# A two-layer encoder trunk in split float32: all 22 channel blocks of the down-projection in the seven-product form

## The chip, the cores and the metric

The kernel runs on one core of one Trainium2 chip. The metric is the device time of one execution, in microseconds (us). Five engines of the core appear below: TensorE (PE; its weight loads are PEld), VectorE (DVE), ScalarE (ACT), GpSimd (POOL) and SyncE (SP). SP and POOL only issue transfers in the stages treated here. Each engine works through its own list of instructions in a fixed order.

## The reference

Two layers, 512 tokens of 1024 channels, float32. A layer is a mixing block (four branches: convolution and three kinds of attention) and then a convolutional feed-forward block. The change concerns the feed-forward block alone:

```
D_MODEL = 1024
SEQ = 512
D_FF = 2816
def _conv_ffn(h, w_up, conv_w, conv_b, w_down):
    u = _depthwise_conv(h @ w_up, conv_w, conv_b)       # width 3 along the tokens
    gate, up = jnp.split(u, 2, axis=-1)
    return (jax.nn.silu(gate) * up) @ w_down
...
        x = x + _conv_ffn(_rmsnorm(x, g_ffn[l]), w_up[l], ffn_conv_w[l], ffn_conv_b[l], w_down[l])
```

So the down-projection is a product of a 512 x 2816 matrix and a 2816 x 1024 one, in each layer.

## The kernel before

**Split float32.** Every float32 operand `x` is cut into `hi = round(x)` in TensorE's reduced float32 (by ACT) and `lo = x - hi` (by DVE), and a product is three matmuls: hi·hi, hi·lo, lo·hi. A matmul works on 128 rows of the contraction and 512 output columns. Weights are cut on the way in: `weights()` loads a unit of 128 x 1024 (512 KB) by SP into a tile `w_raw`, ACT makes `w_hi` of it, DVE makes `w_lo`. There are three `w_hi` and three `w_lo` buffers, so the `w_hi` of a unit can only be made once TensorE has finished the unit three before it. The scheduler gives this work a priority 3000 instructions ahead of its place; where each instruction then stands on its engine is fixed when the program is built.

**Up-projection (`ffn`).** It loops over 22 channel blocks `i`. For each, two units (gate and value half) of 24 matmuls go into two of four PSUM banks `mm`. DVE multiplies the bank by the norm's factors (`U<-mm,RB`), ACT and DVE do the width-3 convolution (`cy`), ACT takes silu (`fth`), DVE multiplies the halves into `fl`, a 128 x 512 tile of the hidden activations. `RB` is known only some time after the first units are done, since it goes through DRAM.

**Down-projection (`down`).** In before, two of the 22 hidden blocks (NK = 2, `kind 'rows'`) are multiplied directly: two units of 24 matmuls, into eight banks. The other 20 go in NP2 = 10 pairs through the seven-product (Strassen-Winograd) scheme. A pair of blocks is a 2 x 2 arrangement of quarters, and seven products of sums of quarters take the place of eight. This needs

- sums of quarters of the weights (`weight_sums`): per pair DVE does four 128 x 512 operations on the two tiles `quad`; POOL has loaded these (two transfers) and stores the results to DRAM (four transfers, `sums`). It runs beside the up-projection, once for every second channel block;
- sums of quarters of the activations, cut into hi and lo (`split_pair`): per pair ACT does three 128 x 512 operations and one of 256 columns, DVE three of 512 and five of 256. In before, four pairs (`EARLY = 4`) are cut beside the up-projection and six in the down-projection.

The first phase of the seven-product form takes two units of 12 matmuls per pair, into eight banks A, B, C, E of 128 x 512 (two of each). In the second phase three of the sums go on to grow, A (`a12`), E (`a22`) and C (`s4`), with one unit of 12 matmuls per two pairs; between them DVE and ACT combine the banks into the result `xt`. In layer 0, `update` then turns the result back and prepares the next layer's norm; in the last layer, the residual (`resT`) is added and `store` writes the output.

**What sets the order on SP.** All loads of `w_raw` stand on SP in one list, with the loads of the residual in the last layer. The weights of the down-projection use four buffers in turn, two named `w_raw` and two named `w_more`; the two `w_more` are the same memory as `quad`, so they become free when the last sums have been stored.

Of the kernel before, what the change touches and what calls it, by code (L numbers as in the profile page):

```python
# [31 lines left out]
NP2 = 10  # L32
NK = NF - 2 * NP2

EARLY = 4
# [28 lines left out]

ORDER = (1, 2, 3, 0)
# [5 lines left out]
def weight_units():  # L71
# [20 lines left out]
    units.extend(('rows', (k0, h), 1024) for h in range(2) for k0 in range(0, NK, 2))  # L92
    units.extend(('quad', NK + 2 * j, 2048) for j in range(NP2))
# [7 lines left out]
def pack_weights(w_in, w_branch, w_out, w_up, w_down):  # L101
    out = np.empty((L, WLEN), np.float32)
    for l in range(L):
        off = 0
        for kind, a, n in UNITS:
# [9 lines left out]
            elif kind == 'rows':  # L115
                k0, h = a
                src = w_down[l][k0 * P:(k0 + 2) * P, h * 512:(h + 1) * 512].reshape(2, P, 512).transpose(1, 0, 2)
# [73 lines left out]
class Trunk:  # L191
# [7 lines left out]
    def weights(self, upto, ahead=3000, parts=1, queue=None):  # L199

        nc = self.nc
        while self.w_emitted < min(upto, len(self.w_list)):
            n, pieces = self.w_list[self.w_emitted]
            with self.tc.high_priority(offset=ahead):
                if n == 0:

                    n = 1024
# [5 lines left out]
                src = pieces()  # L213
                if len(src) == 1:
# [649 lines left out]
    def ffn(self, l, last):  # L864
# [3 lines left out]
        for i in range(4):  # L868
            u = self.fp.tile([P, 514 + (4 * PHASE if i == 3 else 0)], F32, name=f"U{i}", tag=f"U{i}", bufs=1)
# [5 lines left out]
        for i in range(NF):  # L875
# [39 lines left out]
            if i >= NK + 4 and (i - NK) % 4 == 0 and j < EARLY:  # L915
                self.split_pair(F, j, self.got)
# [20 lines left out]
    def last_units(self, l):  # L937
# [7 lines left out]
        for f in (lambda j: quad(j, 2), lambda j: sums(j, 3, 4), lambda j: quad(j, 3)):  # L945
            units.extend(lambda f=f, j=j: [f(j), f(j + 1)] for j in range(0, NP2, 2))
        self.w_list.extend((1024 * (n % 4 < 2), u) for n, u in enumerate(units))
# [7 lines left out]
    def weight_sums(self, l, j):  # L955
# [3 lines left out]
        t3, t2 = (self.fp.tile([P, S], F32, name=f"t{n}", tag=f"s4{n}{j % 2 * 2}", bufs=1) for n in 'hl')  # L959
# [10 lines left out]
    def pair_tags(self, j):  # L970
# [3 lines left out]
        i = NK + 2 * j  # L974
        x = [f"x{n}{d}" for d in range(KT) for n in 'hl']
        own = [f"fh{i}", f"fh{i + 1}"]
        late = [f"fh{NF - 6 + n}" for n in range(6)]
        hi = {NP2 - 3: x[12:14], NP2 - 2: x[14:16], NP2 - 1: ["fh1", "fl1"]}.get(j, own)
        lo = ["lo", "lo"] if j == 0 else [f"fl{i - 2}", f"fl{i - 1}"]
        a = (["e0", "e1"], ["e2", "e3"], late[0:2], late[2:4])[j] if j < EARLY else x[2 * (j - EARLY):][:2]  # L980
        s4 = (["e4", "e5"], late[4:6], ["s4h0", "s4l0"], ["s4h2", "s4l2"], ["fh0", "fl0"])[j // 2]
        return hi + lo + a + s4

    def split_pair(self, F, j, got):
# [3 lines left out]
        i = NK + 2 * j  # L988
        fi, fk = F[i][1], F[i + 1][1]

        def tile(t):
            pool = self.xpool if t[0] == 'x' else self.fp
# [8 lines left out]
        a = self.fp.tile([P, S], F32, name="sum", tag="xr" if j < EARLY else "fth", bufs=2)  # L1001
# [17 lines left out]
    def down(self, F, last):  # L1019
# [9 lines left out]

        got, todo = self.got, list(range(EARLY, NP2))  # L1030

        xt = {}
        names = [('U', i) for i in range(4)] + [('cy', 0), ('cy', 1)] * 2
        for h in range(2):
            pss = [(self.mm if h == 0 else self.aux)() for _ in range(NB)]
            for b in range(NB):
                kind, i = names.pop(0)
                w = 514 + (4 * PHASE if i == 3 else 0) if kind == 'U' else S
                t = self.fp.tile([P, w], F32, name=f"{kind}{i}", tag=f"{kind}{i}", bufs=1 if kind == 'U' else 2)
                xt[b, h] = t[:, :S]  # L1040
                if last:
                    nc.sync.dma_start(xt[b, h], self.resT[b * P:(b + 1) * P, h * S:(h + 1) * S])
            for k0 in range(0, NK, 2):
                w = self.unit()
                for b, k in ([(b, k) for b in range(NB) for k in range(2)] if k0 + 2 == NK else
                             [(b, k) for k in range(2) for b in range(NB)]):
                    t = slice(b * P, (b + 1) * P)
                    prod(pss[b], [f[:, t] for f in F[k0 + k]], w, k, k0 + k == 0, k0 + k == NK - 1)
                    if k0 + k == NK - 1 and last:
# [23 lines left out]
        for b in range(2):  # L1073
            for t in (xt[2 + b, 1], xt[b, 1], xt[2 + b, 0]):
                v.tensor_tensor(t, t, u[b], ALU.add)
            if last:
                self.store(xt, 2 + b, 1)
# [229 lines left out]
```

## Time and profile before

| | |
|---|---|
| time, median of 3 runs | 1565.24 us (1564.06 to 1565.43) |
| time of the profiled execution | 1563.94 us |
| its span, first to last instruction | 1562.2 us |
| TensorE busy / weight loads busy | 1555.9 us / 1295.3 us |
| VectorE / ScalarE / GpSimd busy | 1217.1 / 832.4 / 170.4 us |
| granted TensorE clock, mean of the span | 1.000 |

The profile takes its times from one execution. A busy TensorE is only modelled at the ends of its matmuls, since they overlap: the duration shown for one (0.39 us) is longer than the step from the start of one to the start of the next. Busy times of the other engines are means over stages that differ, so they are read by stage below.

### The profile page before, as it was taken

The numbers are of one execution on the slowest core, as the hardware profiler recorded it, in microseconds if no ns is written. First come the engines' busy times: TensorE is split into PE (matmuls) and PEld (weight loads), VectorE is DVE, ScalarE is ACT, GpSimd is POOL, SyncE is SP. The second block draws the span as 40 slices with busy tenths as digits, with TensorE's granted clock in tenths as the row PEclk, the third lists the DMA queues.
The fourth block names the chain that finished last, engine by engine and source line by source line (L and its number), as shares of the span: only waits on it lengthen the run. The fifth ranks groups of instructions, "written<-read, shape, count | busy, mean of one in ns | idle before, by whom it ended". The sixth has DMA issues, their size and how long they took to land.

```text
span 1562.2 us, 20434 instructions
## 1 busy us (share of the span) xinstructions
PE 1555.9 (100%) x7210; PEld 1295.3 (83%) x7210; DVE 1217.1 (78%) x2073; ACT 832.4 (53%) x1415; POOL 170.4 (11%) x296
## 2 busy tenths in 40 slices
PE   9999999999999999999999999999999999999999
PEld 8888888888888888888888888888888888888887
DVE  6689888765669987796776898887656699987974
ACT  5678767333444444364457687772434444443542
POOL 0002002122001111100001020012120011111000
PEclk9999999999999999999999999999999999999999
DMA  6622222222636655555666322223226477655665
GB/s 232 195 93 82 84 83 82 95 98 93 214 104 213 191 202 188 201 178 195 198 207 184 119 69 86 82 68 109 94 95 217 135 232 217 217 201 192 227 201 163
DMA packets 101238, 239.63 MB, mean 153 GB/s; under 512 B 27280, under 2 KB 29200, under 8 KB 101136
## 3 DMA queue, kind: packets, MB, share of 16 engines
q1 hardware_dynamic: 88240, 194.80, 39.1%
q0 software_dynamic: 12608, 43.01, 7.9%
q8 instruction: 57, 0.93, 0.2%
q10 hardware_dynamic: 288, 0.52, 0.1%
q14 instruction: 45, 0.37, 0.1%
HBM read 199.48 MB, written 33.56 MB: 149 GB/s over the span
## 4 chain that ended last, share of the span: by engine, by line
PE 93%; DVE 3%; ACT 3%; issue 0%; DMA 0%; SPq 0%; ACTq 0%; DVEq 0%
PE mm L246 21%; PE mm L244 21%; PE mm L245 21%; PE aux L1028 3%; PE aux L1027 3%; PE aux L1026 3%; PE mm L440 2%; PE mm L442 2%; PE mm L441 2%; PE mm L1027 2%; PE mm L1026 2%; PE mm L1028 2%; PE aux L710 2%; PE aux L441 1%; PE aux L442 1%; PE aux L440 1%
## 5 line engine op out<-in xcount | busy, mean ns | idle before, releaser
L223 ACT ACTIVATE w_hi<-w_raw 128x1024 fp32r<-128x1024 f32 (+1 forms) x299 | 314.8, 1053 | 354.6 <-PE mm L245 190.9
L244 PE MATMUL mm<-xh,w_hi 128*128 128x512 f32 x1280 | 500.2, 391 | 0.0
L246 PE MATMUL mm<-xh,w_lo 128*128 128x512 f32 x1280 | 499.3, 390 | 0.0
L245 PE MATMUL mm<-xl,w_hi 128*128 128x512 f32 x1280 | 498.8, 390 | 0.0
L225 DVE TENSOR_TENSOR w_lo<-w_raw,w_hi 128x1024 fp32r<-128x1024 f32 (+1 forms) x299 | 365.3, 1222 | 82.9 <-ACT w_hi L223 80.7
L246 PEld LDWEIGHTS mm<-xh,w_lo 128*128 128x128 f32 x1280 | 240.3, 188 | 50.7
L245 PEld LDWEIGHTS mm<-xl,w_hi 128*128 128x128 f32 x1280 | 240.4, 188 | 48.7
L244 PEld LDWEIGHTS mm<-xh,w_hi 128*128 128x128 f32 x1280 | 240.4, 188 | 48.6
L814 POOL TENSOR_TENSOR mx<-mx,t 128x512 f32<-128x512 f32 x44 | 66.9, 1529 | 429.0 <-DVE t L813 327.6
L889 DVE TENSOR_TENSOR U<-mm,RB 128x512 f32<-128x512 f32 x88 | 60.2, 687 | 47.1 <-PE mm L246 37.8
L378 DVE SCALAR_TENSOR_TENSOR cv<-cv,prm 128x512 f32<-128x512 f32 x120 | 93.8, 782 | 0.7
L892 ACT ACTIVATE cy<-U,prm 128x512 f32<-128x512 f32 x88 | 70.8, 807 | 34.3 <-DVE U L889 34.3
L784 DVE TENSOR_TENSOR t<-mm,RB 128x512 f32<-128x512 f32 x64 | 44.0, 687 | 47.8 <-PE mm L246 47.2
L440 PE MATMUL mm<-w_hi,xh 128*128 128x512 f32 x192 | 76.4, 398 | 0.4 <-DVE V L568 0.4
L442 PE MATMUL mm<-w_hi,xl 128*128 128x512 f32 x192 | 75.1, 392 | 0.0
L441 PE MATMUL mm<-w_lo,xh 128*128 128x512 f32 x192 | 75.0, 390 | 0.0
L697 ACT ACTIVATE e<-e,rl 128x256 f32<-128x256 f32 (+2 forms) x96 | 57.4, 598 | 23.3 <-DVE rl L696 23.1
L894 DVE SCALAR_TENSOR_TENSOR cy<-U,prm,cy 128x512 f32<-128x512 f32 x88 | 65.6, 748 | 1.7
L893 DVE SCALAR_TENSOR_TENSOR cy<-U,prm,cy 128x512 f32<-128x512 f32 x88 | 65.5, 746 | 1.3 <-ACT cy L892 1.3
L898 ACT ACTIVATE fth<-cy 128x512 f32<-128x512 f32 x44 | 27.8, 632 | 70.8 <-DVE cy L894 70.8
L690 ACT ACTIVATE e<-e,nm 128x256 f32<-128x256 f32 (+2 forms) x96 | 57.6, 600 | 2.7
L718 DVE TENSOR_TENSOR pt<-aux,pt 128x256 fp32r<-128x256 f32 (+2 forms) x96 | 50.9, 530 | 2.5 <-ACT pt L717 1.2
(276 smaller groups left out, 2595.5 us busy)
## 6 DMA issues: line engine op xcount, KB each, us to landing
w_raw<-W SPq DMA_DIRECT2D x227, 512.0 KB, 3.6
quad<-W POOLq DMA_DIRECT2D x40, 512.0 KB, 5.2
w_raw<-W SPq DMA_DIRECT2D x60, 256.0 KB, 4.1
sums<-quad POOLq DMA_DIRECT2D x40, 256.0 KB, 3.8
w_raw<-sums SPq DMA_DIRECT2D x40, 256.0 KB, 3.9
w_raw<-sums SPq DMA_DIRECT2D x20, 512.0 KB, 3.9
res<-xn SPq DMA_DIRECT2D x24, 256.0 KB, 2.0
xr<-res SPq DMA_DIRECT2D x24, 256.0 KB, 3.9
```

The source lines that it names most:

```text
L223: w = nc.scalar.activation(hi[:, s], raw[:, s], AF.Copy)
L225: nc.vector.tensor_tensor(lo[:, s], raw[:, s], hi[:, s].bitcast(F32), ALU.subtract)
L244: mm(ps, lhsT=wh, rhs=xh, start=start, stop=False)
L245: mm(ps, lhsT=wh, rhs=xl, start=False, stop=False)
L246: self.last_mm = mm(ps, lhsT=wl, rhs=xh, start=False, stop=stop)
L378: self.after_mm(v.scalar_tensor_tensor(acc, u[:, t:t + S], w(t), acc, ALU.mult, ALU.add))
L440: mm(pss[b], lhsT=self.Xh[k][:, t], rhs=hi[:, s], start=k == 0, stop=False)
L441: mm(pss[b], lhsT=self.Xh[k][:, t], rhs=lo[:, s], start=False, stop=False)
L442: self.last_mm = mm(pss[b], lhsT=self.Xl[k][:, t], rhs=hi[:, s], start=False, stop=k == KT - 1)
L1026: mm(ps, lhsT=x[0], rhs=w[0][:, cols], start=start, stop=False, skip_group_check=again)
L1027: mm(ps, lhsT=x[0], rhs=w[1][:, cols], start=False, stop=False, skip_group_check=again)
L1028: self.last_mm = mm(ps, lhsT=x[1], rhs=w[0][:, cols], start=False, stop=stop, skip_group_check=again)
```

## The change

All 22 blocks go through the seven-product form as 11 pairs; the direct part is gone. Six pairs are cut beside the up-projection (after channel blocks 3, 6, 10, 13, 17 and 20) and five in the down-projection. The sums of the weights' quarters are made 11 times for 10, beginning with channel block 0 for block 2. A unit of the second phase holds the blocks of two pairs, and the eleventh pair has a unit of half the size. The combination of the banks is written without the direct part's result, and the residual of the last layer is loaded after the first phase for before it. New homes for the cut activations are found among tiles that are free by then (`xh`, `xl`, `U`, `cy`).

```
-NP2 = 10
-NK = NF - 2 * NP2
-
-EARLY = 4
+NP2 = NF // 2
+
+EARLY = (3, 6, 10, 13, 17, 20)
...
+PHASES = [tuple(range(j, min(j + 2, NP2))) for j in range(0, NP2, 2)]
...
-    units.extend(('rows', (k0, h), 1024) for h in range(2) for k0 in range(0, NK, 2))
-    units.extend(('quad', NK + 2 * j, 2048) for j in range(NP2))
+    units.extend(('quad', 2 * j, 2048) for j in range(NP2))
...
-                if n == 0:
-
-                    n = 1024
+
+                self.w_fast = (self.w_fast + 1) % 4 if n == 0 else 0
+                if n == 0 and self.w_fast in (3, 0):
                     raw = self.fp.tile([P, 1024], F32, name="w_raw", tag="w_more", bufs=2)
...
-            if i > 0 and i % 2 == 0 and i // 2 <= NP2:
+            if i % 2 == 0:
 
                 with self.tc.issue_after(self.last_mm.ins):
-                    self.weight_sums(l, i // 2 - 1)
+                    self.weight_sums(l, i // 2)
...
-            if i >= NK:
-
-                fl = self.fp.tile([P, S], F32, name=f"fl{i}", tag=f"fl{i}", bufs=1)
-                v.tensor_tensor(fl, f, ys[0], ALU.mult)
-                F.append((None, fl))
-            else:
-                fh, fl = (self.fp.tile([P, S], F32R, name=f"{n}{i}", tag=f"{n}{i}", bufs=1) for n in ("fh", "fl"))
-                v.tensor_tensor(f, f, ys[0], ALU.mult)
-                nc.scalar.activation(fh, f, AF.Copy)
-                v.tensor_tensor(fl, f, fh.bitcast(F32), ALU.subtract)
-                F.append((fh, fl))
-            j = (i - NK) // 4 - 1
-            if i >= NK + 4 and (i - NK) % 4 == 0 and j < EARLY:
-                self.split_pair(F, j, self.got)
+
+            fl = self.fp.tile([P, S], F32, name=f"fl{i}", tag=f"fl{i}", bufs=1)
+            v.tensor_tensor(fl, f, ys[0], ALU.mult)
+            F.append(fl)
+            if i in EARLY:
+                self.split_pair(F, EARLY.index(i), self.got)
...
-        for h in range(2):
-            pss = [(self.mm if h == 0 else self.aux)() for _ in range(NB)]
...
-                    prod(pss[b], [f[:, t] for f in F[k0 + k]], w, k, k0 + k == 0, k0 + k == NK - 1)
-                    if k0 + k == NK - 1 and last:
-                        v.tensor_tensor(xt[b, h], pss[b], xt[b, h], ALU.add)
-                    elif k0 + k == NK - 1:
-                        nc.scalar.activation(xt[b, h], pss[b], AF.Copy)
...
+        if last:
+            for b, h in ((2, 1), (3, 1), (0, 1), (1, 1), (2, 0), (3, 0), (0, 0), (1, 0)):
+                nc.sync.dma_start(xt[b, h], self.resT[b * P:(b + 1) * P, h * S:(h + 1) * S])
...
         for banks, x, n, h in ((A, 'a12', 0, 0), (E, 'a22', 2, 0), (C, 's4', 0, 1)):
 
-            end = NP2 - 4 * (banks is C)
-            for j in range(0, end, 2):
+            whole = len(PHASES) - 2 * (banks is C)
+            for js in PHASES[:whole]:
                 w = self.unit()
...
```

Where the built programs differ is shown at three places; names carry the program's numbers, so `fl13` is the hidden block 13 and `w_hi_6440` one particular cut unit. The first is TensorE in layer 0 where the up-projection ends (`xh7`, `xl7` are its last operands) and the down-projection begins. Of before:

```order
L245 MATMUL mm_6389<-xl7_4476,w_hi_6360 128x512
L246 MATMUL mm_6389<-xh7_4475,w_lo_6361 128x512
L1026 MATMUL mm_6445<-w_hi_6391,fh0_4604 128x512
L1027 MATMUL mm_6445<-w_lo_6392,fh0_4604 128x512
L1028 MATMUL mm_6445<-w_hi_6391,fl0_4605 128x512
L1026 MATMUL mm_6445<-w_hi_6391,fh1_4683 128x512
```

Of the change, from the first matmul of the down-projection on, across the first two of its four banks:

```order
L1021 MATMUL mm_6495<-w_hi_6440,pfh0_4864 128x512
L1022 MATMUL mm_6495<-w_lo_6441,pfh0_4864 128x512
L1023 MATMUL mm_6495<-w_hi_6440,plo_4866 128x512
L1021 MATMUL mm_6496<-w_hi_6440,pfh0_4864 128x512
L1022 MATMUL mm_6496<-w_lo_6441,pfh0_4864 128x512
L1023 MATMUL mm_6496<-w_hi_6440,plo_4866 128x512
```

What follows the last matmul of the up-projection is now the first unit of pair 0, with 12 matmuls, where the direct unit had 24; both need the four `mm` banks one after the other.

The second place is DVE in layer 0 at the same time, from the multiplication of the bank of the last but one unit of the up-projection. Of before (`w_lo_6455` belongs to the second direct unit, `w_lo_6518` to the first unit of the seven-product form, and the pair that is cut is that of blocks 10 and 11):

```order
L889 TENSOR_TENSOR U2_4494<-mm_6358,RB_4559 128x512
L225 TENSOR_TENSOR w_lo_6455<-w_raw_6453,w_hi_6454 128x1024
L893 SCALAR_TENSOR_TENSOR cy0_6421<-U2_4494,prm_73,cy0_6421 128x512
L894 SCALAR_TENSOR_TENSOR cy0_6421<-U2_4494,prm_73,cy0_6421 128x512
L1007 TENSOR_TENSOR sum_6495<-fl10_5466,fl11_5561 128x256
L1008 TENSOR_TENSOR fl10_5466<-fl10_5466 128x256
L1009 TENSOR_TENSOR sum_6495<-sum_6495,fl10_5466 128x256
L1013 TENSOR_TENSOR fl11_5561<-fl11_5561,sum_6495 128x256
L1005 TENSOR_TENSOR pfl8_6489<-fl10_5466,pfh10_6487 128x512
L889 TENSOR_TENSOR U3_4497<-mm_6389,RB_4559 128x512
L1005 TENSOR_TENSOR pxl0_6492<-sum_6495,pxh0_6491 128x512
L225 TENSOR_TENSOR w_lo_6518<-w_raw_6516,w_hi_6517 128x1024
```

Of the change, the same stretch (`w_lo_6526` belongs to the second unit of the seven-product form, `w_lo_6544` to the third, and the pair is that of blocks 12 and 13):

```order
L888 TENSOR_TENSOR U2_4494<-mm_6407,RB_4559 128x512
L224 TENSOR_TENSOR w_lo_6526<-w_raw_6524,w_hi_6525 128x1024
L892 SCALAR_TENSOR_TENSOR cy0_6471<-U2_4494,prm_73,cy0_6471 128x512
L1000 TENSOR_TENSOR pfl11_6506<-fl13_5758,pxl0_6504 128x512
L893 SCALAR_TENSOR_TENSOR cy0_6471<-U2_4494,prm_73,cy0_6471 128x512
L1002 TENSOR_TENSOR sum_6511<-fl12_5682,fl13_5758 128x256
L1003 TENSOR_TENSOR fl12_5682<-fl12_5682 128x256
L1004 TENSOR_TENSOR sum_6511<-sum_6511,fl12_5682 128x256
L1008 TENSOR_TENSOR fl13_5758<-fl13_5758,sum_6511 128x256
L888 TENSOR_TENSOR U3_4497<-mm_6438,RB_4559 128x512
L1000 TENSOR_TENSOR pfl10_6505<-fl12_5682,pxh0_6503 128x512
L224 TENSOR_TENSOR w_lo_6544<-w_raw_6542,w_hi_6543 128x1024
```

Behind it stands, in the change, the stretch in which units are half as long as those before and pairs are still cut (the three `w_lo` are those of the eighth, ninth and tenth unit):

```order
L224 TENSOR_TENSOR w_lo_6696<-w_raw_6694,w_hi_6695 128x1024
L1004 TENSOR_TENSOR sum_6625<-sum_6625,fl16_6035 128x256
L1000 TENSOR_TENSOR pfl14_6619<-fl16_6035,pxh2_6617 128x512
L1008 TENSOR_TENSOR fl17_6111<-fl17_6111,sum_6625 128x256
L1000 TENSOR_TENSOR cy0_6622<-sum_6625,cy0_6621 128x512
L1002 TENSOR_TENSOR sum_6681<-fl18_6223,fl19_6299 128x256
L224 TENSOR_TENSOR w_lo_6714<-w_raw_6712,w_hi_6713 128x1024
L1000 TENSOR_TENSOR pxl7_6624<-fl17_6111,pxh7_6623 128x256
L1003 TENSOR_TENSOR fl18_6223<-fl18_6223 128x256
L1004 TENSOR_TENSOR sum_6681<-sum_6681,fl18_6223 128x256
L224 TENSOR_TENSOR w_lo_6754<-w_raw_6752,w_hi_6753 128x1024
```

The list is the same up to the third `w_lo`, but that one is now the third unit's and comes due after two units of 12 matmuls. The stretch between the eighth and the ninth `w_lo` holds the most other work of any between two of the first eleven.

The third place is DVE at the start of the up-projection of layer 0, between the end of the norm (`rstd`) and the first multiplication by `RB`. Of before:

```order
L275 TENSOR_TENSOR rs_q_4543<-rs_q_4543,ms_4540 128x4
L276 SCALAR_TENSOR_TENSOR rstd_4482<-rs_q_4543,rstd_4482 128x4
L225 TENSOR_TENSOR w_lo_4643<-w_raw_4641,w_hi_4642 128x1024
L889 TENSOR_TENSOR U0_4488<-mm_4504,RB_4559 128x512
L889 TENSOR_TENSOR U1_4491<-mm_4561,RB_4559 128x512
```

Of the change:

```order
L275 SCALAR_TENSOR_TENSOR rstd_4482<-rs_q_4543,rstd_4482 128x4
L951 TENSOR_TENSOR t3_4592<-quad_4501,quad_4500 128x512
L952 TENSOR_TENSOR quad_4500<-quad_4500 128x512
L224 TENSOR_TENSOR w_lo_4655<-w_raw_4653,w_hi_4654 128x1024
L953 TENSOR_TENSOR t2_4593<-quad_4501,quad_4500 128x512
L954 TENSOR_TENSOR quad_4501<-quad_4501,t2_4593 128x512
L888 TENSOR_TENSOR U0_4488<-mm_4504,RB_4559 128x512
```

The first sums of the weights' quarters have moved ahead of the first `U<-mm,RB`.

## Rows read from the trace of the kernel before

**Rows 1.** The page's first two parts: busy time, share and number of instructions of each engine; then the granted TensorE clock in 40 equal slices of the span, in tenths (9 is 90% or more).

```profile
PE 1555.9 (100%) x7210; PEld 1295.3 (83%) x7210; DVE 1217.1 (78%) x2073; ACT 832.4 (53%) x1415; POOL 170.4 (11%) x296
...
PEclk9999999999999999999999999999999999999999
```

**Rows 2.** All waits of TensorE in the whole execution: line and tile, whom it waited for, us in total, times, longest.

```profile
PE aux L1158 <- DVE warm L1155: 1.2, 1, 1.2
PE mm L440 <- DVE V L568: 0.4, 1, 0.4
PE aux L510 <- DVE KL L517: 0.3, 1, 0.3
PE aux L672 <- DVE pt L718: 0.3, 1, 0.3
```

**Rows 3.** The timeline of TensorE from the first matmul of the down-projection of layer 0 to the first of its second unit, which is the 25th: start, duration, instruction.

```profile
674.74 0.39 PE L1026 MATMUL mm<-w_hi,fh 128*128 128x512 f32 x1
...
680.18 0.39 PE L1026 MATMUL aux<-w_hi,fh 128*128 128x512 f32 x1
```

**Rows 4.** Busy time by stretch (us from the start of the span: length, then busy time and number of instructions of PE, PEld, DVE, ACT, POOL, the granted clock, the DMA engines' share and GB/s): the up-projection of layer 0, its last stretch, the down-projection of layer 0, and the up-projection of layer 1.

```profile
440.00:670.00 230.00, 230.00 (x1021) 190.59 (x1020) 190.91 (x277) 101.78 (x129) 32.32 (x60) 1.00 0.55 184
670.00:680.00 10.00, 10.00 (x46) 8.29 (x45) 9.90 (x17) 7.56 (x13) 0.17 (x1) 1.00 0.71 248
680.00:770.00 90.00, 90.00 (x399) 74.49 (x398) 66.66 (x103) 44.76 (x55) 0.00 (x0) 1.00 0.56 180
...
1217.00:1447.00 230.00, 230.00 (x1020) 190.61 (x1019) 193.75 (x284) 101.14 (x129) 32.06 (x60) 1.00 0.63 201
```

**Rows 5.** Groups of instructions in the up-projection of layer 0 (440 to 672 us): count, busy us, mean ns of one, idle time of the engine before them and what ended it.

```profile
L225 DVE TENSOR_TENSOR w_lo<-w_raw,w_hi 128x1024 fp32r<-128x1024 f32 x43 | 52.5, 1222 | 8.1 <-ACT w_hi L223 8.0
L960 DVE TENSOR_TENSOR th<-quad 128x512 f32<-128x512 f32 x10 | 6.8, 684 | 0.0
L1005 DVE TENSOR_TENSOR pfl<-fl,pfh 128x512 fp32r<-128x512 f32 x7 | 4.8, 683 | 0.7 <-ACT pfh L1004 0.7
L1007 DVE TENSOR_TENSOR sum<-fl,fl 128x256 f32<-128x256 f32 x4 | 1.7, 426 | 0.1
```

**Rows 6.** The timeline of DVE around the start of the down-projection of layer 0.

```profile
669.86 0.69 DVE L889 TENSOR_TENSOR U<-mm,RB 128x512 f32<-128x512 f32 x1
670.46 1.22 DVE L225 TENSOR_TENSOR w_lo<-w_raw,w_hi 128x1024 fp32r<-128x1024 f32 x1
671.59 0.75 DVE L893 SCALAR_TENSOR_TENSOR cy<-U,prm,cy 128x512 f32<-128x512 f32 x1
...
675.23 0.69 DVE L889 TENSOR_TENSOR U<-mm,RB 128x512 f32<-128x512 f32 x1
...
676.43 1.22 DVE L225 TENSOR_TENSOR w_lo<-w_raw,w_hi 128x1024 fp32r<-128x1024 f32 x1
...
696.36 0.42 DVE L1008 TENSOR_TENSOR fl<-fl 128x256 f32<-128x256 f32 x1
696.69 0.42 DVE L1009 TENSOR_TENSOR sum<-sum,fl 128x256 f32<-128x256 f32 x1
```

**Rows 7.** What ACT waited for from 670 to 770 us, the longest entry (us in total, times, longest), and one timeline row of a `w_hi` behind such a wait.

```profile
ACT w_hi L223 <- PE aux L1028: 20.9, 13, 1.7
...
680.38 1.06 ACT L223 ACTIVATE w_hi<-w_raw 128x1024 fp32r<-128x1024 f32 x1 [0.68 <-PE mm L1028]
```

**Rows 8.** The last two stores of `quad` by POOL and the loads of `w_raw` by SP around the end of the up-projection of layer 0 (start, time on the queue, instruction), and the spread of the time from issue to landing of the loads of `w_raw` from 640 to 700 us.

```profile
667.10 0.55 POOL L966 DMA_DIRECT2D sums<-quad  x1 [3.44 <-DVE quad L961]
669.63 0.54 POOL L966 DMA_DIRECT2D sums<-quad  x1 [0.73 <-DVE quad L963]
...
671.34 0.33 SPq L219 DMA_DIRECT2D w_raw<-W  x1
671.72 1.67 SPq L219 DMA_DIRECT2D w_raw<-sums  x3
...
DMA to landing us min/median/max: 2.8/3.5/5.8
```

**Rows 9.** The page's list of transfers: count, KB each, median us from issue to landing.

```profile
sums<-quad POOLq DMA_DIRECT2D x40, 256.0 KB, 3.8
w_raw<-sums SPq DMA_DIRECT2D x40, 256.0 KB, 3.9
...
res<-xn SPq DMA_DIRECT2D x24, 256.0 KB, 2.0
```

**Rows 10.** The start of the up-projection of layer 0: the first loads of `quad` on POOL, and DVE from the end of the norm to the first multiplication by `RB`.

```profile
397.12 1.12 POOL L953 DMA_DIRECT2D quad<-W  x2
...
444.06 0.16 DVE L276 SCALAR_TENSOR_TENSOR rstd<-rs_q,rstd 128x4 f32<-128x4 f32 x1
447.38 1.22 DVE L225 TENSOR_TENSOR w_lo<-w_raw,w_hi 128x1024 fp32r<-128x1024 f32 x1 [3.15 <-ACT w_hi L223]
451.72 1.29 DVE L889 TENSOR_TENSOR U<-mm,RB 128x512 f32<-128x512 f32 x2 [3.11 <-ACT RB L339]
```

**Rows 11.** The end of the execution: the last matmul and the two last additions on DVE, each followed by a store of its 256 KB tile.

```profile
1557.90 0.39 PE L1028 MATMUL aux<-w_hi,pfl 128*128 128x512 f32 x1
...
1555.61 0.69 DVE L1093 TENSOR_TENSOR cy<-cy,aux 128x512 f32<-128x512 f32 x1 [3.12 <-PE aux L1028]
1558.33 0.69 DVE L1093 TENSOR_TENSOR cy<-cy,aux 128x512 f32<-128x512 f32 x1 [2.03 <-PE aux L1028]
```

More of the change, by code (lines that the diff above doesn't have):

```diff
@@ L213, in weights @@
                 src = pieces()
+                n = sum(p.shape[1] for p in src)
                 if len(src) == 1:
@@ L945, in last_units @@
         for f in (lambda j: quad(j, 2), lambda j: sums(j, 3, 4), lambda j: quad(j, 3)):
-            units.extend(lambda f=f, j=j: [f(j), f(j + 1)] for j in range(0, NP2, 2))
-        self.w_list.extend((1024 * (n % 4 < 2), u) for n, u in enumerate(units))
+            units.extend(lambda f=f, js=js: [f(j) for j in js] for js in PHASES)
+        self.w_list.extend((0, u) for u in units)
     def load_quad(self, l, j):
@@ L1000, in split_pair @@
         bh, bl = (t[:, (lo, hi)[j % 2]] for t in got['b'])
[L1001 removed]
+        a = self.fp.tile([P, S], F32, name="sum", tag="xr" if j < len(EARLY) else "fth", bufs=2)
         def split(h, l, x):
@@ L1068, in down @@
         for b in range(2):
-            v.tensor_tensor(u[b], u[b], B[b], ALU.add)
+            add(u[b], B[b])
         for b in range(2):
-            v.tensor_tensor(xt[2 + b, 1], xt[2 + b, 1], C[b], ALU.add)
-            v.tensor_tensor(xt[2 + b, 1], xt[2 + b, 1], E[b], ALU.add)
-        for b in range(2):
-            for t in (xt[2 + b, 1], xt[b, 1], xt[2 + b, 0]):
-                v.tensor_tensor(t, t, u[b], ALU.add)
-            if last:
+            if last:
+                add(xt[2 + b, 1], C[b])
+            else:
+                v.tensor_tensor(xt[2 + b, 1], u[b], C[b], ALU.add)
@@ L1077, in down @@
+            add(xt[2 + b, 1], E[b])
+        if last:
+            for b in range(2):
+                for t in (xt[2 + b, 1], xt[2 + b, 0], xt[b, 1]):
+                    add(t, u[b])
                 self.store(xt, 2 + b, 1)
         for banks, x, n, h in ((A, 'a12', 0, 0), (E, 'a22', 2, 0), (C, 's4', 0, 1)):
-            end = NP2 - 4 * (banks is C)
-            for j in range(0, end, 2):
+            whole = len(PHASES) - 2 * (banks is C)
+            for js in PHASES[:whole]:
                 w = self.unit()
-                for e in range(2):
+                for e, j in enumerate(js):
@@ L1084, in down @@
                     for b in range(2):
-                        prod(banks[b], got[j + e][x][b], w, e, False, j + e == NP2 - 1, True)
-                if banks is C and not last and j < 4:
-                    for d in (j, j + 1):
+                        prod(banks[b], got[j][x][b], w, e, False, j == NP2 - 1, True)
+                if banks is C and not last and js[0] < 4:
+                    for d in js:
                         self.update(d, self.turn_back(xt, d), self.fp)
-            ws = [self.unit() for _ in range(end, NP2, 2)]
+            ws = [(js, self.unit()) for js in PHASES[whole:]]
@@ L1090, in down @@
             for b in range(2):
-                for j in range(end, NP2):
-                    prod(banks[b], got[j][x][b], ws[(j - end) // 2], j % 2, False, j == NP2 - 1, True)
-                v.tensor_tensor(xt[n + b, h], xt[n + b, h], banks[b], ALU.add)
+                for js, w in ws:
+                    for e, j in enumerate(js):
+                        prod(banks[b], got[j][x][b], w, e, False, j == NP2 - 1, True)
+                t = xt[n + b, h]
+                if last or banks is C:
+                    add(t, banks[b])
+                elif banks is E:
+                    v.tensor_tensor(t, u[b], banks[b], ALU.add)
+                else:
+                    nc.scalar.activation(t, banks[b], AF.Copy)
```

56 lines of the change are left out of this document (23 added, 33 removed).

## Prediction

> **What bounds the kernel now.** Read the waits of TensorE first [rows 2]: over the whole execution it waits 2.2 us for others, all outside the feed-forward blocks, and the clock is granted in full throughout [rows 1]. So the stage that changes is bound by the row of matmuls alone. What one of them costs is not the 0.39 us that the timeline shows as its duration, since they overlap; it is the step from start to start. From the first matmul of the down-projection to the 25th it is 680.18 - 674.74 = 5.44 us [rows 3], or 0.2267 us each. Next come the stretches [rows 4]: VectorE is busy for 190.9 of 230 us beside the up-projection, 9.9 of 10 us at the change-over to the down-projection, and 66.7 of 90 us in it. It is the engine that could start to matter, and the change-over is the place. ScalarE has room everywhere.
>
> **What is removed and added on TensorE.** Per layer, the direct part has 2 blocks x 4 token blocks x 2 halves = 16 products of three matmuls, 48 in all. An eleventh pair has 7 products x 2 banks x 3 = 42. Six fewer per layer and twelve in both, all of 512 columns: 12 x 0.2267 = 2.72 us. Nothing else on TensorE changes in number.
>
> One rule speaks about this price. The Trainium skill (TensorE: Matmul & The Clock Gate, Back-to-back issue gap) gives about 131 ns for a matmul of 512 columns in a sustained row and about 216 ns for a lone one. By the first the gain would be 1.6 us, by the second 2.6 us. The 227 ns step of this trace is longer than both; it decides.
>
> **More sums and more cutting beside the up-projection.** A sum of a pair's weights is four DVE operations of 0.684 us [rows 5], so the eleventh adds 2.7 us per layer. In the new list all of the first sum stands between the end of the norm and the first `U<-mm,RB`. There DVE now does one `w_lo` of 1.22 us between 444.2 and 451.7 us and otherwise waits, for ACT and for `RB` [rows 10]; `quad` was issued at 397 us. Its cover is that wait of more than 6 us. Without the cover it would delay the first evacuations by 2.7 us, while four banks of 5.44 us each stand between them and TensorE. Cost: nothing.
>
> Cutting a pair is five operations of 256 columns (0.42 us) and three of 512 (0.68 us): 4.2 us [rows 5]. Two more pairs beside the up-projection make 8.3 us, less two subtractions of 0.68 us that the direct blocks needed. Together DVE goes from 190.9 to about 200.5 us of 230 in layer 0 and from 193.8 to 203.4 in layer 1. That leaves 26 us, and the pairs' cuts stand apart in the list. Nothing waits for a cut within 25 us, and a `w_lo` has two units, 10.9 us, from the release of its buffer until TensorE wants it. Cost: nothing; the upper bound, if all 9.6 us per layer came through, is taken up below.
>
> **The change-over.** This is the step to follow unit by unit. Before, the up-projection is followed by two units of 5.44 us; now at once by units of 12 matmuls, 2.72 us. In steps from start to start, a `w_lo` takes DVE 1.13 us (670.46 to 671.59), an operation of 512 columns 0.60 (669.86 to 670.46), one of 256 columns 0.33 (696.36 to 696.69), a convolution step about 0.75 [rows 6]. Lay the new list on these. Up to the third `w_lo` it has the same work as before, so that starts at 676.43 [rows 6] and ends at 677.65. TensorE needs it at the second matmul of the third unit: 674.74 + 2 x 2.72 + 0.23 = 680.41. Slack 2.8 us. Going on down the list, the `w_lo` of units four to eleven end at about 680.1, 682.9, 685.7, 688.4, 691.1, 694.5, 696.7 and 699.6 us; they are due at 683.1, 685.9, 688.6, 691.3, 694.0, 696.7, 699.5 and 702.2. The slack stays between 2.2 us (ninth unit, behind 0.33 x 3 + 0.60 x 2 of cutting) and 3.0 us.
>
> The chain ahead of DVE keeps pace. `w_hi` of a unit can start when the unit three before is done, 0.2 us later (680.38 behind 680.18) and takes 1.06 us [rows 7]: for the fourth unit 677.7 to 678.7, and the list has its `w_lo` at 678.9. That wait of ACT for TensorE, 20.9 us in one entry [rows 7], is no loss; it shows that three buffers set the pace.
>
> The loads of the third and fourth unit wait for the stores of `quad`. These are issued at 667.10 and 669.63 [rows 8] and land 3.8 us later [rows 9], at 670.9 and 673.4; the loads need 3.9 us more, to 675.2 (issued at 671.34) and 677.3. Just in time for `w_hi`. If store and load both took the 5.8 us of the slowest load shown [rows 8], the fourth unit would be 3.9 us late, 0.9 us beyond its slack, and 1.8 us over both layers. I take zero, since the medians fit, and keep 1.8 us as the upper end. The `mm` banks are wanted in the same order and at the same times as before.
>
> **The rest of the down-projection.** Six pairs were cut there, now five, in 22 units of 2.72 us; 5 x (5 x 0.33 + 3 x 0.60) = 17.3 us of cutting at the steps above and 22 x 1.13 = 24.9 us of `w_lo` make 42 us of 60, and the first pair cut there is wanted 32 us after the start. Three more units per layer, each half as large, add 0.6 us each on ACT and DVE, beside TensorE. Eight evacuations of the direct part go. In the last layer the residual's loads stand behind waits for the seventh to tenth pair on SP, and loads of weights queue behind them; these are wanted some 8 us later and land in 3.9 us [rows 9]. Cost: nothing, at most 4 us once, a whole load.
>
> **The end.** The last addition starts 0.04 us after the last matmul has ended (1557.90 + 0.39) and then comes one store [rows 11]. Now the store before it has 9 x 0.2267 = 2.0 us of head start for 2.7; a 256 KB store lands in 2.0 us [rows 9]. Between 0 and 0.7 us, taken as 0.
>
> **Sum.** 1563.94 - 2.72 = 1561.2 us for the profiled execution. It is 1.3 us under the median of the runs, 1565.24; from the median, 1562.5 us, 0.17% less. About 0.2%, here 3.1 us, is what a measurement of this kernel can tell from no change. So the forecast falls just inside "same".
>
> **Rivals.**
>
> *TensorE has room, and the matmuls were not the limit.* Weight loads are busy for 83% of the span, matmuls for 100% [rows 1]. The matmuls' share says nothing on its own, as their ends are modelled. If the limit were elsewhere, taking twelve away would leave 1565.2 us. Against it: a step of 0.2267 us, and no wait [rows 2]. The Trainium skill (Perfetto Trace Analysis, Identifying the Most-Contended Engine) holds that matmul busy time is no measure of the distance to the roofline and that weight-load busy time is; by that rule a sixth of the time is free. Chance 0.08.
>
> *A little is lost at the change-over or behind the residual's loads*: up to 1.8 us and 4 us by the bounds above, so most of the gain is given back; between 1562.9 and 1565.3 us. Chance 0.10.
>
> *Slower: the change-over stalls in both layers.* The mechanism is the load of the fourth unit, which waits for a store that waits for the last sum, with all later loads of SP behind it. It decides from the point where the loss is 2.72 + 3.13 = 5.85 us, 2.9 us per layer: the load then lands 5.9 us later than I put it, 9.8 us after its issue for the 5.8 us of the slowest shown [rows 8]. With 11.6 us, twice the slowest, the loss is 7.7 - 3.0 = 4.7 us per layer and the time 1565.24 - 2.72 + 9.4 = 1571.9 us. Should all of the extra 9.6 us of DVE per layer come through, it would be 1581.7. For it: the DMA engines are at 71% at this place and four units' loads fall into some 8 us. Against it: DVE's own list has the slack. Chance 0.07.
>
> *More than the sum is gained*, below 1562.1 us with no stall: no term for it in the trace but the runs' spread of 1.4 us. Chance 0.03 beside that spread.
>
> **How the numbers follow.** The forecast has 0.72. Its own range is 1561.3 to 1562.9 us, the runs' spread moved down by 2.72; a quarter of it, 0.18, lies beyond 0.2%. Faster: 0.18 + 0.03 = 0.21. Same: 0.54 + 0.08 + 0.10 = 0.72. Slower: 0.07. The range 1561.1 to 1565.5 us takes in the forecast, the little losses and "no gain", and leaves out the slower rival and the extra gain, 0.10.
>
> **What would show it.** The new profile should have 12 matmuls fewer (7198), a step of 0.2267 us in the down-projection, no wait of TensorE between 670 and 770 us, and the third unit's `w_lo` at the same 676.4 us. DVE should be busy for about 200 us of the 230 beside the up-projection, with four operations on `quad` between 444 and 452 us. I am wrong if TensorE waits for `w_lo` or `w_hi` around 683 us or 1461 us, if a load of `w_raw` on SP stands behind a residual's load for longer than 8 us, or if the first matmul of the down-projection waits for a bank.

## The result, and the profile after

The changed kernel takes 1566.41 us (median of 18 runs, 1565.79 to 1569.75), the kernel before 1564.02 us in the same series (18 runs, 1563.64 to 1565.43). The ratio is 1.0016, with a 95% interval from 1.0009 to 1.0023: some 2.5 us slower, where 2.7 us faster was forecast. The profiled execution took 1567.13 us with a span of 1565.4 us, 3.2 us more than the span of before.

The page's line of busy times answers [rows 1], and all waits of TensorE answer [rows 2]:

```profile
PE 1558.2 (100%) x7198; PEld 1292.9 (83%) x7198; DVE 1220.3 (78%) x2083; ACT 833.9 (53%) x1419; POOL 176.8 (11%) x308
...
PE aux L1151 <- DVE warm L1148: 1.2, 1, 1.2
PE aux L440 <- DVE w_lo L224: 0.8, 1, 0.8
PE mm L439 <- DVE V L567: 0.4, 1, 0.4
PE aux L1022 <- DVE w_lo L224: 0.3, 1, 0.3
PE aux L509 <- DVE KL L516: 0.3, 1, 0.3
PE aux L671 <- DVE pt L717: 0.3, 1, 0.3
```

The twelve matmuls are gone, yet TensorE is busy 2.3 us longer. Of the two new waits, that of 0.3 us (L1022) stands at 781 us, at the end of layer 0's down-projection; that of 0.8 us (L440) stands ahead of 380 us, and by 440 us both kernels are level within 0.2 us. Nothing waits at the change-over.

The stretches of [rows 4], columns as there, from the changed kernel (up-projection of layer 0, the change-over, the down-projection of layer 0, the up-projection of layer 1):

```profile
440.00:670.00 230.00, 230.00 (x1018) 190.54 (x1019) 198.04 (x294) 102.62 (x132) 35.71 (x66) 1.00 0.58 193
670.00:680.00 10.00, 10.00 (x45) 8.16 (x45) 8.38 (x14) 6.88 (x12) 0.01 (x1) 1.00 0.69 215
680.00:770.00 90.00, 90.00 (x393) 73.20 (x392) 61.67 (x94) 43.55 (x52) 0.24 (x4) 1.00 0.62 192
1217.00:1447.00 230.00, 230.00 (x1020) 190.42 (x1019) 199.37 (x299) 101.39 (x131) 34.60 (x64) 1.00 0.66 209
```

VectorE has 198.0 and 199.4 us of work beside the up-projections, for the 200.5 and 203.4 forecast, and the granted clock stays at 1.00. But from 680 to 770 us stand 393 matmuls of TensorE where 399 stood. The timeline shows the same, the first matmul of the down-projection and the 151st:

```profile
674.59 0.40 PE L1021 MATMUL mm<-w_hi,pfh 128*128 128x512 f32 x1
...
709.45 0.39 PE L1021 MATMUL mm<-w_hi,U 128*128 128x512 f32 x1
```

The step is (709.45 - 674.59) / 150 = 0.2324 us, in place of the 0.2267 of [rows 3], and no row between them shows a wait. Summed over all steps under 0.3 us from 674 to 790 and from 1452 to 1563 us (the down-projections, and a few matmuls behind the first of them), the surplus over 0.2267 is 2.46 and 2.43 us. So: 12 x 0.2267 = 2.7 us saved, 4.9 us lost in the pace, about 0.8 us in longer gaps at the end of layer 0's down-projection and just behind it, 0.3 us scattered between the two stretches: 3.3 us more, for 3.2 in the spans.

### The profile page after: what moved, and what is told of

Read it like the earlier page. It is cut to its first block, busy times and chain, and to the rows that moved or that the text cites. A ratio compares the mean times of both kernels' runs of the same rounds, so it can differ in the third digit from the quotient of the medians.

```text
span 1565.4 us, 20475 instructions
## 1 busy us (share of the span) xinstructions
PE 1558.2 (100%) x7198; PEld 1292.9 (83%) x7198; DVE 1220.3 (78%) x2083; ACT 833.9 (53%) x1419; POOL 176.8 (11%) x308
## 4 chain that ended last, share of the span: by engine, by line
PE 93%; DVE 3%; ACT 3%; issue 0%; DMA 0%; SPq 0%; ACTq 0%; DVEq 0%
PE mm L243 21%; PE mm L245 21%; PE mm L244 21%; PE aux L1022 3%; PE aux L1023 3%; PE aux L1021 3%; PE mm L439 2%; PE mm L441 2%; PE mm L440 2%; PE mm L1023 2%; PE mm L1022 2%; PE mm L1021 2%; PE aux L709 2%; PE aux L440 1%; PE aux L441 1%; PE aux L439 1%
## 5 line engine op out<-in xcount | busy, mean ns | idle before, releaser
L222 ACT ACTIVATE w_hi<-w_raw 128x1024 fp32r<-128x1024 f32 (+1 forms) x305 | 318.3, 1044 | 353.2 <-PE mm L244 191.3
L440 PE MATMUL mm<-w_lo,xh 128*128 128x512 f32 x192 | 74.9, 390 | 0.0
```

Source lines behind the costliest of these rows:

```text
L222: w = nc.scalar.activation(hi[:, s], raw[:, s], AF.Copy)
L440: mm(pss[b], lhsT=self.Xh[k][:, t], rhs=lo[:, s], start=False, stop=False)
```

## Experiments

**What changed the pace?** One line of the diff, which the excerpt above leaves out, is about neither matmuls nor cutting. `U3` had 96 unused floats behind it:

```diff
-            u = self.fp.tile([P, 514 + (4 * PHASE if i == 3 else 0)], F32, name=f"U{i}", tag=f"U{i}", bufs=1)
+            u = self.conv_tile(f"U{i}")
...
+    def conv_tile(self, tag, dt=F32):
+        w = 514 if tag[0] == 'U' else S
```

A matmul has a stationary operand, which the weight load puts into TensorE ahead of it, and a moving one, which it then reads; both lie in SBUF, the core's on-chip memory. In the built programs, `w_hi` and `w_lo` (the moving operands of the down-projection) lie in every partition at addresses that leave 448 when divided by 512. In the kernel before, so did the cut activations (the stationary ones); in the changed kernel the tiles allocated behind `U3` all leave 64, 384 bytes lower. Three theories of the slower pace: the addresses; denser traffic into SBUF; the order of the work, in units of 12 matmuls.

Run `a_pad` puts the padding back:

```diff
-        w = 514 if tag[0] == 'U' else S
+        w = 514 + (4 * PHASE if tag == 'U3' else 0) if tag[0] == 'U' else S
```

> The changed kernel with the 96 unused floats (384 bytes) behind U3 put back, and nothing else. Address theory (a matmul goes at 0.2267 us only where the stationary operand that is loaded next lies at the same address modulo 512 bytes as the moving operand being read; the change shifted the whole ffn pool by 384 bytes against the weights): the down-projection's 461 and 485 matmuls go at 0.2267 again in place of 0.2319, which takes away 2.46 + 2.43 us, less some 0.1 us for U1 to U3, which stay off the residue: 1566.4 - 4.8 = 1561.6 us, about 2.4 us under the kernel before. The wait of about 0.8 us for the last half unit's w_lo near 780 us stays. Traffic theory (the denser cutting and loading in the down-projection slows TensorE's reads): the same work and traffic, so the step stays at 0.232 and the time at 1566.4 us. Order theory (units of 12 matmuls with another moving tile each cost a little at every change): also 1566.4 us.

Run `b_nopad` is the kernel before with `514` in both places where it had `514 + (4 * PHASE if i == 3 else 0)`.

> The kernel before with U3's 96 unused floats taken away, and nothing else. Address theory: the down-projection's 936 matmuls of 512 columns go at about 0.232 us in place of 0.2267, save those with a stationary operand in an x tile: about 0.8 x 936 x 0.0057 = 4.3 us to 936 x 0.0057 = 5.3 us more, 1568.3 to 1569.3 us. Traffic and order theory: nothing that they speak of is touched, 1564.0 us and a step of 0.2267.

Runs `a_pad104` and `a_pad32` are `a_pad` with `4 * PHASE + 8` and `32` for `4 * PHASE`.

> The changed kernel with 104 floats behind U3, 32 bytes more than the padding of the kernel before. Address theory: the stationary operands lie 32 bytes off the moving ones modulo 512; the trace after has eight such matmuls (homes in U1), which went at 0.238 us, so the step in the down-projection is about 0.238 for four in five of 924 matmuls: 0.8 x 924 x 0.0113 = 8.4 us over the padded kernel, about 1570 us. If it were a coarser alignment (384 bytes restored is what counts, a little more or less is not): about 1561.6 us. Traffic and order theory: 1566.4 us.

> The changed kernel with 32 floats (128 bytes) behind U3: the stationary operands then lie 256 bytes off the moving ones modulo 512, in place of 128. Address theory with a period of 512 bytes: slow still, 0.2328 us as in the 56 matmuls of the kernel before that stand 256 bytes off, so about 1566.5 to 1567 us. With a period of 256 bytes: 0.2267 and about 1561.6 us. Traffic and order theory: 0.232, 1566.4 us, so this run tells the period and not the theories.

Measured: `a_pad` 1563.97 us (0.9994 of before, 0.9985 to 1.0003), `b_nopad` 1568.97 us (1.0025, 1.0015 to 1.0035), `a_pad104` 1568.11 us (1.0021, 1.0012 to 1.0030), `a_pad32` 1565.04 us in one run. How many matmuls TensorE starts in 60 us in the middle of each down-projection tells more (length, busy time and number of PE, granted clock, DMA share, GB/s). The kernel before:

```profile
700.00:760.00 60.00, 60.00 (x267) 1.00 0.60 193
1480.00:1540.00 60.00, 60.00 (x267) 1.00 0.68 216
```

The changed kernel:

```profile
700.00:760.00 60.00, 60.00 (x261) 1.00 0.62 194
1480.00:1540.00 60.00, 60.00 (x260) 1.00 0.75 244
```

`a_pad`:

```profile
700.00:760.00 60.00, 60.00 (x266) 1.00 0.65 198
1480.00:1540.00 60.00, 60.00 (x266) 1.00 0.78 249
```

`b_nopad`:

```profile
700.00:760.00 60.00, 60.00 (x261) 1.00 0.61 190
1480.00:1540.00 60.00, 60.00 (x262) 1.00 0.66 209
```

`a_pad104`, then `a_pad32`:

```profile
700.00:760.00 60.00, 60.00 (x260) 1.00 0.63 194
1480.00:1540.00 60.00, 60.00 (x259) 1.00 0.78 243
```

```profile
700.00:760.00 60.00, 60.00 (x266) 1.00 0.63 197
1480.00:1540.00 60.00, 60.00 (x266) 1.00 0.78 249
```

The padding alone switches the pace, in both kernels and both ways. Traffic is not the cause: `a_pad` moves more per second (249 against 244 GB/s) and is quicker. Order is not: `b_nopad` has the old order and is slow. It is the addresses that count. (The padding moves the operands of the other engines too; the table that follows ties the step to those of the matmul.)

Starts from the traces laid beside addresses from the built programs give the step by the distance of the stationary operands, the one in use and the next, from the moving one (modulo 512 bytes, the shorter way round; steps under 0.26 us between two matmuls of a down-projection, both layers):

| distance | kernel | matmuls | mean step, ns |
|---|---|---|---|
| 0 | before | 930 | 226.7 |
| 0 | `a_pad` | 868 | 227.1 |
| 256 bytes | `a_pad32` | 549 | 226.9 |
| 128 bytes | after | 552 | 232.6 |
| 0 | after | 156 | 228.1 |
| 128 bytes | `b_nopad` | 682 | 232.5 |
| 32 bytes | `a_pad104` | 552 | 233.1 |
| 0 | `a_pad104` | 156 | 230.0 |
| 32 bytes for the next one alone | `a_pad104` | 92 | 237.8 |
| 32 bytes for the one in use alone | `a_pad104` | 90 | 229.7 |

Two rows are of the same execution of the changed kernel: 156 matmuls whose stationary operands lie at distance 0 (most of them in tiles of another pool, which did not move) step 4.5 ns sooner than the 552 at 128 bytes.

So in the down-projection 256 bytes count as none, which the expectation of `a_pad32` left open, and 32 bytes cost as much as 128. The 56 matmuls at 0.2328 us which that expectation names are no counterexample that can be used: each stands ahead of an operation of another kind (with `cst`, 128 columns), not in a row of like matmuls. The 238 ns expected of `a_pad104` hold only where the next operand alone is off; the step with only the one in use off took 229.7, so that the two average 233.8, hardly more than the row of 32 bytes. So the down-projections of `a_pad104` lost about 4.9 us against those of `a_pad`, not the 8.4 expected, and it took 1568 and not 1570 us. How the hardware brings all this about, no run shows. The Trainium skill (SBUF — State Buffer, A bandwidth-pool intuition that's wrong (but worth ruling out)) gives TensorE a second, independent read port for loading weights; by that the place of the stationary operand would make no difference. The runs differ, and they decide.

**Where the other half of the gain went.** `a_pad` won back 2.4 us of the 4.8 expected. Its first 150 steps are back, 34.20 us with two gaps of 0.14 us together:

```profile
674.96 0.39 PE L1021 MATMUL mm<-w_hi,pfh 128*128 128x512 f32 x1
...
709.16 0.39 PE L1021 MATMUL mm<-w_hi,U 128*128 128x512 f32 x1
```

The two stretches together have 0.64 us of surplus left (`U1` to `U3` are off by 32 to 96 bytes still). The rest are waits. Steps over 0.3 us cost, beyond those of the kernel before, 0.95 us from 674 to 790 us, 0.54 in the up-projection of layer 1 and 0.79 in its down-projection. By the waits of TensorE in `a_pad` (behind 380 us):

```profile
PE aux L1022 <- DVE w_lo L224: 0.3, 1, 0.3
PE aux L671 <- DVE pt L717: 0.3, 1, 0.3
PE mm L243 <- DVE U L888: 0.3, 1, 0.3
PE mm L1022 <- DVE w_lo L224: 0.2, 1, 0.2
```

The first stands at 780 us, the second is the old one of the attention [rows 2], the others stand at 1235 and 1476 us. Three moves were tried on `a_pad`, one by one and together: `p_half` puts the half-size unit of a pass of the second phase first, `p_odd` makes the first sums of weights one channel block later, `p_space` spreads the late cuts over every second pair. In this order, with a second piece of `p_half` at the end:

```diff
-PHASES = [tuple(range(j, min(j + 2, NP2))) for j in range(0, NP2, 2)]
+PHASES = [(0,)] + [(j, j + 1) for j in range(1, NP2, 2)]
...
-            if i % 2 == 0:
+            if i == 1 or i > 0 and i % 2 == 0:
...
-            if todo:
+            if todo and j % 2 == 0:
...
-                if banks is C and not last and js[0] < 4:
-                    for d in js:
+                if banks is C and not last and js[0] in (1, 3):
+                    for d in (js[0] - 1, js[0]):
```

> The padded kernel with three moves: the first sums of weights one step later (i = 1 in place of 0), the five late pairs cut at every second pair in place of every one, and the half-size unit of each second-phase pass first in place of last. Wait theory (what the padded kernel falls short of its forecast are TensorE's waits that the slow step had covered: about 0.9 us at the end of layer 0's down-projection, 0.55 us near 1234 us, 0.85 us at the two change-overs): these go, so 1563.97 - 2.3 = 1561.7 us, 0.9982 of the kernel before, with the sum of steps over 300 ns from 380 us on back to that of the kernel before. Rival (VectorE or the loads are short in the whole down-projection, so that a wait taken away comes back at another place): waits of 1 to 2 us elsewhere and a time of 1563 to 1564 us.

> The padded kernel with the half-size unit of each second-phase pass first in place of last. Wait theory: no wait for w_lo at 779 us nor at 784 us, 0.9 us less than the padded kernel; the waits at 1234 and 1475 us stay. Rival: the residual's updates push VectorE's cutting back as before, and a wait of about 0.8 us stands at the last units all the same.

> The padded kernel with the first sums of weights one step later. Wait theory (the stores of the sums and the later landing of the row of scales on GpSimd's queue hold up RB in layer 1): the broadcast load of the row is issued at about 1226 us again in place of 1228.6, RB is written at about 1231 in place of 1233.3, and the wait at 1234 us goes: 0.55 us less than the padded kernel. Rival (RB is late for another reason, such as TensorE's start of the layer): RB stays at about 1233 us and the wait stays.

> The padded kernel with the five late pairs cut at every second pair of the first phase. Wait theory (VectorE has about 6.1 us of work for 5.4 us of products while it cuts a pair for each pair multiplied, and falls behind): no waits for w_lo between 1455 and 1480 us, about 0.7 us less in layer 1 and 0.14 in layer 0. Rival (the loads of the weights are late, not the cutting): the waits for w_lo stay at 1458 and 1475 us.

All three together, `p_all`, took 1565.1 us (1.0004, 0.9995 to 1.0013): no gain, and waits of 1.6 and 0.6 us at new places, as the rival has it, though its number was 1563 to 1564 us. The single runs (1565.5, 1564.58 and 1564.37 us) say little as times, but each trace shows its wait go, or part of it, and another come or grow.

- `p_half`: no wait at 779 us, but one of 1.6 us at 786 us, for a bank:

```profile
PE aux L439 <- DVE cy L1047: 1.6, 1, 1.6
```

- `p_odd`: the cause of the wait at 1234 us was on GpSimd's queue. In `a_pad` the load of the row of scales (`raw<-row`) is issued 2.65 us later than in the kernel before, behind a store of sums and a slower landing of the row; without the sums `RB` follows 1.66 us earlier and TensorE does not wait there. The kernel before, `a_pad`, then `p_odd`:

```profile
1225.97 0.54 POOL L335 DMA_DIRECT2D raw<-row  x1 [2.68 <-DMA row<-rstd]
```

```profile
1223.67 0.55 POOL L957 DMA_DIRECT2D sums<-t  x1
1228.62 0.54 POOL L334 DMA_DIRECT2D raw<-row  x1 [4.40 <-DMA row<-rstd]
...
1233.27 1.11 ACT L338 ACTIVATE RB<-raw 128x512 f32<-128x512 f32 x1 [8.35 <-DMA raw<-row]
```

```profile
1226.95 0.54 POOL L334 DMA_DIRECT2D raw<-row  x1 [2.90 <-DMA row<-rstd]
...
1231.61 1.12 ACT L338 ACTIVATE RB<-raw 128x512 f32<-128x512 f32 x1 [6.20 <-DMA raw<-row]
...
1291.21 0.71 DVE L916 STREAM_TRANSPOSE xn<-xr 128x512 f32<-128x512 f32 x1 [1.53 <-DMA resT<-xn]
```

  Its last row is the new wait: VectorE's order has moved, a transposed residual tile waits 1.53 us for the store of an earlier one, the next `w_lo` is late and TensorE waits 0.6 us at 1296 us.
- `p_space`: the gaps at 1458 and 1461 us in layer 1 are gone, that at 1475 us (0.2 us of wait) stays. VectorE's surplus of cutting was part of the cause, not all. The waits at 779 and 1234 us grew, from 0.3 to 0.6 and from 0.3 to 0.5 us.

Next, whether the late work at 775 to 780 us comes of SyncE's queue. `p_res` moves the residual's loads there to GpSimd's queue, `p_res_space` and `p_res_odd_space` add the moves of those names (the second edit stands in two places):

```diff
-        nc.sync.dma_start(xr, self.xres[d])
+        (queue or nc.sync).dma_start(xr, self.xres[d])
...
-                        self.update(d, self.turn_back(xt, d), self.fp)
+                        self.update(d, self.turn_back(xt, d), self.fp, nc.gpsimd)
```

> The padded kernel with the down-projection's loads of the residual (xr) on GpSimd's queue in place of SyncE's. Queue theory (the load of the third residual tile stands 5.8 us behind the weights' loads on SyncE's queue, VectorE waits 3.8 us for it at 771.7 us, and the cut of the last half unit comes late behind it): the load lands within 3 us, VectorE's wait falls under 1 us, TensorE's waits at 779 and 784 us go, 0.9 us less than the padded kernel. Rival (the transfers share the bandwidth, whatever their queue): VectorE's wait stays over 3 us and TensorE's waits stay.

> The same with the five late pairs cut at every second pair. Wait theory: 0.9 us less at the end of layer 0 and at most 0.7 us less at the change-over of layer 1, 1562.4 to 1563.0 us, 0.9987 of the kernel before. Rival (waits move as in the run with three moves): 1563.9 us or more.

> The same again with the first sums of weights one step later as well. Wait theory: also 0.55 us less near 1234 us, 1561.9 to 1562.5 us, 0.9984 of the kernel before. Rival (waits move: with this move the kernel of an earlier run waited 0.9 us near 1296 us instead, where a transposed residual tile waited for the store of the one before): 1563.5 us or more.

They took 1565.42 us (one run), 1565.02 us (1.0001, 0.9992 to 1.0010) and 1566.70 us (1.0010, 1.0000 to 1.0019): three misses of the queue and wait theories, and each time the outcome that the rival names. The third residual tile decides it, first in `a_pad`, then in `p_res`, its load, its transposes on TensorE and its addition on VectorE:

```profile
769.68 0.42 SPq L853 DMA_DIRECT2D xr<-res  x1
...
775.50 0.69 DVE L855 TENSOR_TENSOR xn<-mm,xr 128x512 f32<-128x512 f32 x1 [3.83 <-DMA xr<-res]
```

```profile
769.75 0.54 POOL L853 DMA_DIRECT2D xr<-res  x1 [99.24 <-DVE xn L855]
...
771.66 1.03 PE L1103 MATMUL mm<-cst,U 128*128 128x128 f32 x8
...
775.60 0.69 DVE L855 TENSOR_TENSOR xn<-mm,xr 128x512 f32<-128x512 f32 x1 [3.75 <-PE aux L1023]
```

On SyncE's queue the load lands 5.7 us after its issue, on GpSimd's 5.6 us: at 775.38 us in both, and the addition follows within 0.22 us. The last row names TensorE, but the transposes that the addition reads were done by 772.7 us; it is the load that VectorE waits for, in both kernels. So SyncE's queue was not what held it up. In the kernel before the same load took 3.4 us; why it takes longer here no run shows (the DMA engines are busy for 0.83 of the time from 769 to 776 us in `a_pad`, for 0.71 in the kernel before).

That left the order on VectorE. In `p_half` the add that empties the last bank (L1047) stands behind two cuts of weights and a sum of squares:

```profile
784.36 1.22 DVE L224 TENSOR_TENSOR w_lo<-w_raw,w_hi 128x1024 fp32r<-128x1024 f32 x1 [0.20 <-ACT w_hi L222]
785.50 0.68 DVE L308 TENSOR_TENSOR sqacc<-sqacc,sq 128x512 f32<-128x512 f32 x1
786.10 1.22 DVE L224 TENSOR_TENSOR w_lo<-w_raw,w_hi 128x1024 fp32r<-128x1024 f32 x1
787.24 0.68 DVE L1047 TENSOR_TENSOR cy<-cy,aux 128x512 f32<-128x512 f32 x1
```

Run `p_half_first` gives that add the norm's priority:

```diff
-                if last or banks is C:
+                if last:
                     add(t, banks[b])
+                elif banks is C:
+                    with self.first():
+                        add(t, banks[b])
```

> The padded kernel with the half-size unit first in each second-phase pass, as in the earlier run, and the add that empties the last bank of the pass put ahead in VectorE's queue (it is given the priority that the norm's own steps have, so that one cut of weights stands ahead of it in place of two and a sum of squares). Queue theory (the 1.6 us at 786 us in the earlier run was TensorE waiting for a bank whose add stood 3 us back in VectorE's order): that wait falls under 0.3 us and nothing takes its place in layer 0; span 1563.7 - 1.6 = 1562.1 us, some 1563.3 us, 0.999 of the kernel before. Rival (VectorE is short of time there, whatever the order): the wait becomes one for w_lo or xl of 1 us or more between 780 and 795 us, and the time stays at 1564.5 us or more.

It took 1563.25 us, 0.9990 of the kernel before (0.9981 to 0.9999), with a span of 1561.6 us. The add now starts right behind one cut:

```profile
782.38 1.21 DVE L224 TENSOR_TENSOR w_lo<-w_raw,w_hi 128x1024 fp32r<-128x1024 f32 x1
783.51 0.68 DVE L1047 TENSOR_TENSOR cy<-cy,aux 128x512 f32<-128x512 f32 x1
```

and TensorE's waits behind 380 us are these, none of them at the end of layer 0's down-projection (the last stands at 697 us, where `p_half` has it too):

```profile
PE mm L243 <- DVE U L888: 0.5, 1, 0.5
PE aux L671 <- DVE pt L717: 0.3, 1, 0.3
PE mm L1022 <- DVE w_lo L224: 0.2, 1, 0.2
```

So it was not time that VectorE lacked there: it still waits 2.66 us for the third residual tile, and putting one addition ahead was enough. The time and the wait came out as the theory of VectorE's order (there called queue theory) has them. This version is faster than the changed kernel, and by 0.1% than the kernel before, at the edge of what can be told; from `a_pad` it cannot be told apart. The wait of 0.5 us for `RB` at 1234 us remains, and the 12 matmuls' 2.7 us are not all in hand.

## Why the prediction was wrong

- **The step that failed** is the first working: "Six fewer per layer and twelve in both, all of 512 columns: 12 x 0.2267 = 2.72 us. Nothing else on TensorE changes in number." The number was right (7198). But the sum priced only the twelve that go and took 0.2267 us for the 924 that stay, a price that hung on the addresses of [rows 3]'s operands. They stepped at 0.2319 us on average: 4.8 us for which there was no term. The lost padding stood in the diff, and I gave it no term. No rival covered it: the slower one had the right sign, but by a stall at the change-over, and TensorE did not wait there. Of the signs named beforehand the 7198 matmuls and the missing wait came, the step of 0.2267 us did not.
- **The base of the forecast** was the median of three runs, 1565.24 us, and happened to be high; 18 runs give 1564.02. From there the sum gives 1561.3 us, so the sum missed by 5.1 us, not by the 3.9 that the forecast of 1562.5 shows.
- **TensorE has room** (rival) is refuted: a pace 2.2% slower cost the kernel 4.4 us in `b_nopad`, with nothing else touched.
- **More sums and cutting beside the up-projection, cost nothing**: right for VectorE (198.0 of 230 us, for 200.5). Wrong for the queue that I did not walk along: the sums' stores stand on GpSimd ahead of the load for `RB`. In the changed kernel TensorE was late enough for it not to matter; at the full pace it cost 0.5 us in layer 1 (`a_pad`).
- **The change-over**: no wait, as forecast, but with less to spare. The third unit's `w_lo` came at 677.85 us for 676.43, since its load from `sums` landed late:

```profile
676.76 1.06 ACT L222 ACTIVATE w_hi<-w_raw 128x1024 fp32r<-128x1024 f32 x1 [1.79 <-DMA w_raw<-sums]
...
677.85 1.22 DVE L224 TENSOR_TENSOR w_lo<-w_raw,w_hi 128x1024 fp32r<-128x1024 f32 x1 [1.56 <-ACT w_hi L222]
```

  At the full pace the gaps of this stage cost 0.1 us in layer 0, at 697 us (the ninth unit, where I put the smallest slack, 2.2 us), and 0.8 us in layer 1 (`a_pad`): that slack was put too high.
- **The rest of the down-projection, cost nothing**: mis-sized by about 0.8 us. The half-size unit comes last in layer 0, in the stretch in which VectorE also has the next layer's norm to do, and waits for the third residual tile.
- **The end**: right, the last addition again starts 0.04 us behind the last matmul's end (1561.55 against 1561.11 + 0.40).

## What to carry to other kernels

When one engine sets the pace, price the instructions that stay as well as those that go: a change to tile shapes or pools moves addresses, and 5 ns on each of 924 matmuls outweighed twelve matmuls. Treat an odd padding in a tuned kernel as a load-bearing line until a run without it says otherwise, and compare matmuls per 60 us before and after before looking for waits. And when a slow pace is mended, expect waits that it had covered; here one of them went by putting the right operation first on the other engine, where moving work had only moved the waits. And check a wait's named cause against the times of everything that the instruction reads: the row of `p_res` names the wrong one.

## What the runs showed of the hardware

- In the down-projection a reduced float32 matmul of 512 columns stepped at 226.7 to 227.1 ns where its stationary operand and the next lay 0 or 256 bytes from the moving one modulo 512, and at 232.5 to 233.1 ns where they lay 32 or 128 bytes off, at a granted clock of 1.00. Where only the next stationary operand lay 32 bytes off, it was 237.8 ns, and 229.7 ns where only the one in use did. Among matmuls at distance 0 that stand between others off it, the mean rose to 228.1 (after) and 230.0 ns (`a_pad104`).
- The slow pace shows in no wait and in no share: TensorE is at 100% and its weight loads at 83% in both kernels.
- Moving the residual's load from SyncE's queue to GpSimd's did not make it land earlier: 5.7 and 5.6 us after its issue, at 775.38 us in both.
